# Two attention layers on one core: sums over partitions and the turn of the maxima on VectorE instead of TensorE

## The chip, the cores and the metric

The kernel runs on one core of one Trainium2 chip, as one program. The metric is the device time of one execution in microseconds (us), lower is better. A core has five engines that work beside each other, each through its own instructions in order: TensorE (PE, matrix products, with the weight loads shown as PEld), VectorE (DVE), ScalarE (ACT), GpSimd (POOL) and SyncE (SP), which here issues DMAs. Data lies in SBUF, 128 partitions of a row each; TensorE writes to PSUM, and the other engines read both.

## The reference

Two transformer layers over 1024 latent tokens with 256 context tokens, width 1024. Each normalizes and modulates its input, projects it, runs attention of 16 heads, multiplies by a gate and projects back. Layer 0 has grouped queries (4 key heads), layer 1 latent attention: its queries are expanded from 384 columns, normalized per head (96 columns) and rotated in 32 of them. Cut to what the change touches:

```python
def gqa_attend(q, k, v):
    s = jnp.einsum('bqhgd,bkhd->bhgqk', q, k).astype(jnp.float32) * (GQA_HEAD_DIM ** -0.5)
    p = jax.nn.softmax(s, axis=-1).astype(v.dtype)
    return jnp.einsum('bhgqk,bkhd->bqhgd', p, v)
...
    def q_heads(q_a, n):
        q = (rms_norm(q_a, p["q_a_norm"]) @ p["w_q_b"]).reshape(B, n, MLA_HEADS, MLA_NOPE + MLA_ROPE)
        q = rms_norm(q, p["q_norm"])
        return jnp.split(q, [MLA_NOPE], axis=-1)
```

The softmax needs, for each query, the maximum of its scores and the sum of their exponentials over all keys. Latent queries read 1280 keys, context queries 256.

## The kernel before

`Attention` (L312) runs a layer's units one after another; `run` (L694) is the loop. A unit is one pair of heads' share: 1024 query columns (two halves of 512) against the keys, in tiles `kt` of 128 keys, ten for a latent unit and two for a context unit. Layer 0 (`WIDE`) has 16 latent and 4 context units, the latter fifth, tenth and last two; layer 1 has 16 latent units. Keys lie on the partitions and queries in the columns, so that the exponentials `p` can go straight into the second product.

One unit, step by step:

- For each `kt`, `scores_by_halves` (L560) makes the scores `st` in PSUM in several products, of which the last one adds a shift: minus the query's maximum, taken from a row. ACT takes the exponential, `p` (L567).
- Beside each `kt`, TensorE makes scores of a later unit with the queries on the partitions, `mx` (L436 and L441 in layer 0, one tile of 1024 columns per `kt`; L402 and L412 in layer 1, two tiles of 512). DVE reduces them to a maximum per query (L445, L447; L404, L415), and L465 joins these to `m`, 128 x 8. Layer 0 has two PSUM buffers for `mx`, layer 1 three of half the size.
- `turn` (in `do_shift`, L469 to L481) brings `m` into a row: TensorE transposes it into a buffer of `mx` (L474), DVE copies it to `crow` in SBUF (L476), and two DMAs on SP put it in the row of the shift.
- POOL adds up the tiles `p` over `kt` in `acp` (L601), 128 x 1024; for the last four `kt` of a latent unit DVE first adds pairs (`acd`, L587), and POOL adds those.
- `do_av` (L617) multiplies `p` with the values, 20 products of 2 x 512 columns a latent unit, into `avt` or `av`.
- `total` (in `finish`, L655 to L669) sums `acp` over the partitions: four pairs of products with the constant `twos` (L662) on TensorE, into a buffer of `mx` or `av`; DVE transposes the result (L666) and takes reciprocals (L667), 128 x 8; a DMA writes them to `rrow` in memory, from where `spread` fetches them over the partitions, and POOL multiplies the output with them and with the gate (L681, L682).

A unit's total comes in the following unit: in layer 0 after the first `kt` of that unit's AV (`postponed`, `second`), in layer 1 before its AV. Totals of units that end while context units run are kept until the next latent unit, so two can come at once.

In `run`, a manual schedule keeps PE, DVE and ACT in the order of the code; the framework places POOL's and SP's instructions. Elsewhere the framework orders all engines.

The query stage of layer 1 comes between the two attentions: two `staged` loops (L1833, L1836) of eight steps, one per 128 tokens, with `q_expand` (L1772) in each. For each of two halves of 384 columns it makes the projection `mm`, a sum of squares `qss`, a reciprocal root `q_rs` (L118 on DVE, then POOL), two multiplications from PSUM into `t` (L1788) and `qt` (L1793), an addition on POOL, and the multiplication `t` by `q_rs` (L1796). `q_store` transposes the result on TensorE (`tp`, L1806) and splits it (`tl`, L88) for storing.

Of the kernel before, what the change touches and what calls it, by code (L numbers as in the profile page):

```python
# [10 lines left out]
F32 = mybir.dt.float32  # L11
# [26 lines left out]
def hybrid_kernel(ctx: ExitStack, tc: tile.TileContext, ins: dict, out: bass.AP):  # L38
# [12 lines left out]
    def pad(pool, size):  # L51

        pool.tile([P, size // 4], F32, name="pad", tag="pad", bufs=1)

    pad(sm_pool, 352)

    ident = const.tile([P, P], F32, name="ident")
    make_identity(nc, ident)
# [1 line left out]
    pool.memset(mhalf, -0.5)  # L60
    twos = const.tile([P, 32], F32, name="twos")
    pool.memset(twos, 2.0)


    x1d = dram.tile([NT, D], F32, name="x1d")
# [16 lines left out]
    def in_order(engine):  # L82

        return tc.manual_schedule(engines={engine})

    def split(hi, lo, src):
        act.copy(hi, src)
# [224 lines left out]
    class Attention:  # L312
        def __init__(self, l, units, ops):
            self.l, self.units, self.ops = l, units, ops
            self.state = {}
            self.vcache = {}
            self.kcache = {}
            self.sm = sm_pool
            self.step = 0
            self.deferred = []  # L320
            self.totals = []
            self.turns = []
            self.started = 0
            self.done = 0
            self.todo = []
            self.last_lat = [u for u in units if u["kind"] == "lat"][-1]
# [133 lines left out]
        def do_shift(self, u):  # L460

            s = self.state[id(u)]
            if u["kind"] == "lat":
                m = self.sm.tile([P, 8], F32, name="m1", tag="m1")
                dve.reduce_max(m, s["m"], axis=AX.X)  # L465
            else:
                m = s["m"][:, :, 0]

            def turn():  # L469
                if not WIDE[self.l]:  # L470
                    t = self.ps_m.tile([P, 512], F32, name="mx", tag="mx")[:8, :P]
                else:
                    t = self.ps_m.tile([P, 1024], F32, name="mx", tag="mx")[:8, :P]
                pe.transpose(t, m, ident)  # L474
                r = self.rows[self.units.index(u) % 2] if WIDE[self.l] else self.sm.tile([8, P], F32R, name="crow", tag="crow", bufs=1)
                dve.tensor_copy(r, t)  # L476
                if HALVES[self.l]:
                    for n in range(2):
                        sp.dma_start(raw(s["crow"][n]), raw(r[4 * n:4 * n + 4, :]))
                else:  # L480
                    sp.dma_start(raw(s["crow"]), raw(r))  # L481

            self.turns.append((self.units.index(u), turn))

# [117 lines left out]
                s["sum"] = t  # L602
            s["total"] = ([s["sum"]] if held else []) + last

        def do_av(self, u, group, ps, second=None):

            s = self.state[id(u)]
            kts = u["kts"]
            if group[0] == kts[0]:
                if not WIDE[self.l]:  # L610
                    s["av"] = self.ps_o.tile([P, 512], F32, name="av", tag="av")
                s["v"] = self.load_v(u)
            for kt, p in zip(group, ps):
                if second and kt == kts[1]:
                    second()
                for n in range(2):
                    pe.matmul(s["av"][64 * n:64 * n + 64, :], lhsT=s["v"][:, kt, u["vc"]:u["vc"] + 64],  # L617
                              rhs=p[:, n * 512:(n + 1) * 512], start=kt == kts[0], stop=kt == kts[-1])
            if group[-1] == kts[-1]:
                self.finish(u)  # L620
# [12 lines left out]
        def finish(self, u):  # L633
            l, op, sm = self.l, self.op, self.sm
            s = self.state.pop(id(u))
            lat = u["kind"] == "lat"
            o = op.tile([P, 512], F32, name="os", tag="os")
            act.copy(o, s["av"])

            def parts(dst):  # L640

                if lat:
                    r = slice(64 * u["par"], 64 * u["par"] + 64)
                    return [(slice(64 * n, 64 * n + 64), dst[u["pair"], r, 512 * n:512 * n + 512], lambda t: t)
                            for n in range(2)]
                g = u["g"]
                return [(slice(0, P), dst[2 * g:2 * g + 2, :, NL:].rearrange("a p n -> p a n"),
                         lambda t: t.rearrange("p (a n) -> p a n", a=2))]

            rrow = self.rd.tile([2, 512], F32, name="rrow", tag="rrow")  # L650

            rb = sg = None
            cr = sm.tile([P, 8], F32, name="cr", tag="cr")

            def total(gap):  # L655
                if WIDE[l]:
                    t = self.ps_m.tile([P, 1024], F32, name="mx", tag="mx")[:, :512]
                else:
                    t = s["av"] if u is not self.units[-1] and not HALVES[l] else self.ps_m.tile([P, 512], F32, name="mx", tag="mx")
                for i, part in enumerate(s["total"]):  # L660
                    for q in range(4):
                        pe.matmul(t[32 * q:32 * q + 32, :256], lhsT=twos, rhs=part[:, q * 256:q * 256 + 256],  # L662
                                  start=i == 0, stop=i == len(s["total"]) - 1)

                tr = t[:, 256:]
                dve.transpose(tr, t[:, :256].rearrange("p (a b) -> p b a", b=8))  # L666
                dve.reciprocal(cr, tr.rearrange("p (b a) -> p b a", a=32)[:, :, 0])  # L667
                sp.dma_start(rrow.rearrange("o (a b) -> (o a) b", b=8), cr)
                self.later(*((d + gap, fn) for d, fn in zip(self.ops["gaps"], (spread, scale, store))))  # L669

            def spread():
                nonlocal rb, sg
                rb = op.tile([P, 512], F32, name="rb", tag="rb", bufs=1)
                sg = op.tile([P, 512], F32, name="sg", tag="sg", bufs=1)
                for rows, src, view in parts(sgd[l]):
                    sp.dma_start(view(sg[rows, :]), src)
                for n in range(2):
                    sp.dma_start(rb[64 * n:64 * n + 64, :], rrow[n:n + 1, :].broadcast_to([64, 512]))

            def scale():  # L680
                pool.tensor_mul(rb, rb, sg)  # L681
# [12 lines left out]
        def run(self, lead, ahead, extra, tail):  # L694
# [3 lines left out]
            with tc.manual_schedule(engines={mybir.EngineType.PE, mybir.EngineType.DVE, mybir.EngineType.Activation}):  # L698
                for t, u in enumerate(self.units):
# [18 lines left out]
                    for group in (kts[:cut], kts[cut:]):  # L718
# [30 lines left out]
                            self.add_up(u, *(([], sums) if cut else (sums, [])))  # L749
                        if final:  # L750
                            self.run_deferred(self.step + 2)
                        def sum_totals():
                            gap = 0
                            while self.totals and (whole or late or final):
                                self.totals.pop(0)(gap)
                                gap += 3

                        postponed = WIDE[self.l] and whole and group[0] == kts[0]
                        if not postponed:
                            sum_totals()  # L760
                        if t % 2 and end:
                            if parts:
                                parts()
                            parts = extra.pop(0)() if extra else None
                        self.do_av(u, group, ps, sum_totals if postponed else None)
                        self.step += (2 + len(group)) // 3
                gap = 0
                while self.totals:
                    self.totals.pop(0)(gap)
                    gap += 3  # L770
            self.run_deferred(self.step)

# [521 lines left out]
    def l0_open(at, st):  # L1294
        pool_ = st.enter_context(tc.tile_pool(name="shift0", bufs=1, **right))
        at.minus = pool_.tile([P, 4, P], F32R, name="minus")
        at.shift = pool_.tile([P, 512], F32R, name="shift")
        at.rows = [pool_.tile([8, P], F32R, name=f"crow{i}") for i in range(2)]
        pool.memset(raw(at.shift), 0.0)
        for i in range(4):  # L1300
            a, b = (ident[:, j:j + 1].broadcast_to([P, P]) for j in (i, 64 + i))
# [421 lines left out]
    with ExitStack() as st:  # L1723
# [47 lines left out]

        def q_expand(tt, c, w, lat):  # L1772
            qah, qal = lat
            held = []
            for q4 in range(2):
                ns = slice(384 * q4, 384 * q4 + 384)
                ps = ps_mm.tile([P, 512], F32, name="mm", tag="mm")
# [14 lines left out]
                for s_ in range(2):  # L1792
                    dve.tensor_tensor(t2[:, :, :, s_, :], p5[:, :, :, 1 - s_, :],  # L1793
                                      sv[:, :, s_, :].unsqueeze(1).broadcast_to([P, 4, 2, 8]), op=ALU.mult)
                pool.tensor_add(t1v[:, :, 64:96], t1v[:, :, 64:96], t2.rearrange("p h a s d -> p h (a s d)"))
                dve.tensor_tensor(t1v, t1v, rs.unsqueeze(2).broadcast_to([P, 4, 96]), op=ALU.mult)  # L1796
                held.append(t1)
            return held

        def q_store(tt, c, held):  # L1800
# [29 lines left out]
            return fn  # L1830

        todo_g = list(slices)
        staged(range(TL), q_compress, q_latent, later, expand(0), gate((0, 0, 0, 0, 0, 1, 1, 1)), later, store(0))  # L1833
        wqb.append(load_weight(ins["l1_w_q_b"], 3, 768, 768))
        wg1 = load_weight(w_in1, KT, 1184, 512)
        staged(range(TL), q_fetch, expand(1), gate((0, 1, 0, 1, 0, 1, 1, 1)), store(1))  # L1836
    stQ.close()
    stT.close()
    at.open_early(stE)
# [86 lines left out]
```

## Time and profile before

| | us |
|---|---|
| median of 3 runs | 1669.49 (1668.81 to 1670.78) |
| the profiled execution | 1668.65 |
| its span in the trace | 1666.9 |
| TensorE matmuls L662, `acp`, 272 of them | 21.3 busy |
| TensorE transpositions L474, 36 of them | 9.7 busy |
| VectorE L666, 36 of them | 16.0 busy |
| VectorE L667, 36 of them | 7.5 busy |
| VectorE L476, 36 of them | 9.8 busy |
| VectorE L1796, 32 of them | 20.0 busy, 24.3 idle before them |

A row of the profile's timeline gives the start in us from the span's start, the duration, the engine, the line, the operation and the tiles it writes and reads. A number in brackets is the time for which the engine had been idle before, with what it waited for. Rows of the same kind are merged (x4), and their durations overlap a little at the edges, since an instruction starts before the one ahead has quite ended; what a piece of work takes of its engine is therefore read from start to start. A busy time in the page sums durations.

### The profile page before, as it was taken

How to read it: one execution, taken by the hardware profiler on the slowest of the kernel's cores; microseconds unless marked ns; L12 is line 12 of the kernel's file. 1: busy time of each engine (PE TensorE's matmuls, PEld its weight loads, DVE VectorE, ACT ScalarE, POOL GpSimd, SP SyncE). 2: the span in 40 equal slices, each digit the busy share in tenths (PEclk: the TensorE clock that was granted, in tenths of full speed). 3: DMA queues.
4: the chain of work that ended last, by engine and by line, in shares of the span. 5: the costliest groups of instructions: out<-in, count | busy, mean ns of one | idle time of the engine just before them, and what ended most of it. 6: DMA issues, size and time to landing. Idle time of an engine off the chain costs nothing.

```text
span 1666.9 us, 27267 instructions
## 1 busy us (share of the span) xinstructions
PE 1636.5 (98%) x10236; PEld 1187.3 (71%) x10236; DVE 1043.3 (63%) x1660; ACT 640.1 (38%) x944; POOL 949.1 (57%) x624
## 2 busy tenths in 40 slices
PE   8999999999999999999999999999999999999998
PEld 5776668885555555558888898887676766767587
DVE  3774553457788777625675667755777777677231
ACT  4642222224455544432234543331443534435310
POOL 2673441118899898842235555450767878778521
PEclk9999999999999999999999999999999999999999
DMA  9547856532252432156424776767456564563451
GB/s 311 181 131 251 254 164 197 155 97 59 77 146 69 120 87 77 51 151 208 133 71 131 231 208 189 226 203 195 113 130 157 117 147 112 130 141 73 128 172 68
DMA packets 221116, 244.21 MB, mean 147 GB/s; under 512 B 23160, under 2 KB 160616, under 8 KB 220984
## 3 DMA queue, kind: packets, MB, share of 16 engines
q1 hardware_dynamic: 220560, 242.36, 52.1%
q8 instruction: 81, 1.33, 0.3%
q14 instruction: 51, 0.42, 0.1%
q10 hardware_dynamic: 424, 0.11, 0.0%
HBM read 168.62 MB, written 73.63 MB: 145 GB/s over the span
## 4 chain that ended last, share of the span: by engine, by line
PE 86%; DVE 6%; POOL 3%; issue 3%; ACT 1%; DMA 1%; ACTq 0%; SPq 0%; DVEq 0%; POOLq 0%
PE st L560 19%; PE avt L617 9%; PE av L617 8%; PE mm L94 8%; PE mm L96 7%; PE mm L95 7%; PE mx L402 4%; PE y L94 4%; PE y L96 4%; PE y L95 4%; PE mx L436 2%; PE pm L201 1%; PE mx L662 1%; DVE wb L137 1%; DVE m L445 1%
## 5 line engine op out<-in xcount | busy, mean ns | idle before, releaser
L567 ACT ACTIVATE p<-st 128x1024 f32<-128x1024 f32 x328 | 335.9, 1027 | 155.8 <-PE st L560 140.4
L601 POOL TENSOR_TENSOR acp<-acp,p 128x1024 f32<-128x1024 f32 x128 | 305.4, 2386 | 8.3 <-ACT p L567 0.4
L404 DVE TENSOR_REDUCE m<-mx 128x1 f32<-128x512 f32 x256 | 175.6, 691 | 95.1 <-PE mx L402 89.4
L445 DVE TENSOR_REDUCE m<-mx 128x1 f32<-128x1024 f32 x128 | 150.4, 1219 | 70.3 <-PE mx L436 69.7
L601 POOL TENSOR_TENSOR acp<-p 128x1024 f32<-128x1024 f32 x34 | 81.5, 2399 | 176.5 <-ACT p L567 176.5
L617 PE MATMUL avt<-p,v 128*64 128x512 f32 x672 | 152.5, 598 | 0.6 <-DVE crow L476 0.3
L601 POOL TENSOR_TENSOR acp<-acp,acd 128x1024 f32<-128x1024 f32 x60 | 141.9, 2365 | 14.7 <-DVE acd L587 11.5
L587 DVE TENSOR_REDUCE acd<-p 128x512 f32<-128x1024 f32 x124 | 144.8, 1221 | 6.9 <-ACT p L567 6.9
L617 PE MATMUL av<-p,v 128*64 128x512 f32 x640 | 141.1, 595 | 0.0
L137 POOL TENSOR_TENSOR wb<-wraw,wa 128x512 fp32r<-128x512 f32 (+3 forms) x65 | 87.7, 1364 | 78.3 <-ACT wa L158 78.3
L94 PE MATMUL mm<-wa,hh 128*128 128x512 f32 (+2 forms) x336 | 126.5, 376 | 2.0 <-ACT hh L974 2.0
L560 PE MATMUL st<-QH,KH 64*128 64x512 f32 x320 | 122.7, 407 | 0.1
L96 PE MATMUL mm<-wa,hl 128*128 128x512 f32 (+2 forms) x336 | 121.0, 360 | 1.4 <-DVE hl L977 1.4
L95 PE MATMUL mm<-wb,hh 128*128 128x512 f32 (+2 forms) x336 | 120.4, 358 | 0.0
L560 PE MATMUL st<-QH,KL 64*128 64x512 f32 x320 | 118.3, 391 | 0.0
L560 PE MATMUL st<-QL,KH 64*128 64x512 f32 x320 | 117.8, 390 | 0.0
L94 PE MATMUL y<-wa,oh 128*128 128x512 f32 (+1 forms) x296 | 114.2, 386 | 0.6 <-ACT oh L813 0.6
L95 PE MATMUL y<-wb,oh 128*128 128x512 f32 (+1 forms) x296 | 113.7, 384 | 0.0
L96 PE MATMUL y<-wa,ol 128*128 128x512 f32 (+1 forms) x296 | 113.6, 384 | 0.0
L617 PEld LDWEIGHTS av<-p,v 128*64 128x64 f32 x640 | 44.5, 137 | 88.3 <-issue 87.6
L617 PEld LDWEIGHTS avt<-p,v 128*64 128x64 f32 x672 | 44.9, 136 | 86.9 <-issue 80.6
L94 PE MATMUL mm<-hh,wa 128*128 128x512 f32 (+1 forms) x264 | 103.2, 391 | 0.2 <-DVE qt L1793 0.2
(247 smaller groups left out, 4015.8 us busy)
## 6 DMA issues: line engine op xcount, KB each, us to landing
mraw<-in_l_w_mod SPq DMA_DIRECT2D x64, 256.0 KB
wraw<-in_l_w_in SPq DMA_DIRECT2D x28, 512.0 KB
KH<-k1h SPq DMA_DIRECT2D x32, 320.0 KB
KL<-k1l SPq DMA_DIRECT2D x32, 320.0 KB
rb<-rrow SPq DMA_DIRECT2D x72, 128.0 KB
mraw<-in_l_w_mod SPq DMA_DIRECT2D x16, 512.0 KB
QA<-q0h SPq DMA_DIRECT2D x32, 256.0 KB
wraw<-in_l_w_out SPq DMA_DIRECT2D x16, 512.0 KB
```

The source lines that it names most:

```text
L94: pe.matmul(ps, lhsT=lh(k), rhs=rh(k), start=first and i == 0, stop=False)
L95: pe.matmul(ps, lhsT=lh(k), rhs=rl(k), start=False, stop=False)
L96: pe.matmul(ps, lhsT=ll(k), rhs=rh(k), start=False, stop=last and i == len(ks) - 1)
L137: eng.tensor_sub(lo, a, b)
L402: pe.matmul(held["m"][:, cs], lhsT=q[:, t * P:(t + 1) * P], rhs=k[:, ks], start=j == 0, stop=j == len(pairs) - 1)
L404: dve.reduce_max(s["m"][:, i, n:n + 1], held["m"], axis=AX.X)
L445: dve.reduce_max(s["m"][:, i, 0:1], m, axis=AX.X)
L560: pe.matmul(ps[:, n * 512:(n + 1) * 512], lhsT=lh, rhs=rh, start=j == 0, stop=j == last)
L567: act.activation(p, ps, AF.Exp, scale=self.ops["scale"])
L587: dve.reduce_sum(t[:, ns], p2.rearrange("p a n -> p n a")[:, ns, :], axis=AX.X)
L601: pool.tensor_add(t, a, b)
L617: pe.matmul(s["av"][64 * n:64 * n + 64, :], lhsT=s["v"][:, kt, u["vc"]:u["vc"] + 64], rhs=p[:, n * 512:(n + 1) * 512], start=kt == kts[0], ...
```

## The change

- Two tiles are new, shared by all: `square`, 128 x 32, and `turned`, 128 x 128. A pad of the pool they lie in shrinks by as much. `turn_squares` transposes the four 32 x 32 blocks of `square` (partitions 0, 32, 64 and 96) into 32 partitions of `turned`, side by side.
- `turn` no longer uses TensorE: DVE copies `m` to the first eight columns of `square`, transposes the squares, and the two DMAs read `turned`.
- `total_by_squares` replaces `total` but for the layer's last units (`late` or `final`): DVE reduces `acp` with `apply_transpose` into `square`, transposes the squares, adds the four, doubles, takes reciprocals of 32 x 32, and the DMA reads these. It holds for 17 totals of layer 0 and 15 of layer 1; three and one remain on TensorE.
- Totals come ahead of AV in layer 0 too; `second` and `postponed` go.
- The query stage runs in written order on DVE, and `q_expand` multiplies by `q_rs` behind both halves.

The diff, cut:

```diff
-    pad(sm_pool, 352)
+    pad(sm_pool, 224)
...
+    square = sm_pool.tile([P, 32], F32R, name="square", tag="square", bufs=1)
+    pool.memset(raw(square), 0.0)
+    turned = sm_pool.tile([P, P], F32, name="turned", tag="turned", bufs=1)
...
+    def turn_squares(dst):
+
+        for g in range(4):
+            dve.transpose(dst[:, 32 * g:32 * g + 32], raw(square[32 * g:32 * g + 32, :]))
...
             def turn():
-                if not WIDE[self.l]:
-                    t = self.ps_m.tile([P, 512], F32, name="mx", tag="mx")[:8, :P]
-                else:
-                    t = self.ps_m.tile([P, 1024], F32, name="mx", tag="mx")[:8, :P]
-                pe.transpose(t, m, ident)
-                r = self.rows[self.units.index(u) % 2] if WIDE[self.l] else self.sm.tile([8, P], F32R, name="crow", tag="crow", bufs=1)
-                dve.tensor_copy(r, t)
...
+                at_ = 32 * (self.units.index(u) % 2)
+                r = turned[at_:at_ + 32, :]
+                dve.tensor_copy(square[:, :8], m)
+                turn_squares(r)
+                for n in range(2):
+                    sp.dma_start(raw(s["crow"][n]), r[4 * n:4 * n + 4, :])
...
+            def total_by_squares(gap):
+                part, = s["total"]
+                dve.tensor_reduce(raw(square), part.rearrange("p (b r) -> p b r", r=32), axis=AX.X, op=ALU.add,
+                                  apply_transpose=True)
+                sums = turned[64:96, :]
+                turn_squares(sums)
+                i = self.sums % 4
+                self.sums += 1
+                c = turned[96:128, 32 * i:32 * i + 32]
+                dve.reduce_sum(c, sums.rearrange("q (g r) -> q r g", r=32), axis=AX.X)
+                dve.tensor_scalar(c, c, 2.0, None, op0=ALU.mult)
+                dve.reciprocal(c, c)
+                sp.dma_start(rrow.rearrange("o (a b) -> (o a) b", b=32), c)
+                then(gap)
...
-                        postponed = WIDE[self.l] and whole and group[0] == kts[0]
-                        if not postponed:
-                            sum_totals()
+                        gap = 0
+                        while self.totals and (whole or late or final):
+                            self.totals.pop(0)(gap, not (late or final))
+                            gap += 3
...
-                        self.do_av(u, group, ps, sum_totals if postponed else None)
+                        self.do_av(u, group, ps)
...
                 pool.tensor_add(t1v[:, :, 64:96], t1v[:, :, 64:96], t2.rearrange("p h a s d -> p h (a s d)"))
+                held.append(t1)
+                todo.append((t1v, rs))
+            for t1v, rs in todo:
                 dve.tensor_tensor(t1v, t1v, rs.unsqueeze(2).broadcast_to([P, 4, 96]), op=ALU.mult)
-                held.append(t1)
...
-        staged(range(TL), q_compress, q_latent, later, expand(0), gate((0, 0, 0, 0, 0, 1, 1, 1)), later, store(0))
+        with in_order(mybir.EngineType.DVE):
+            staged(range(TL), q_compress, q_latent, later, expand(0), gate((0, 0, 0, 0, 0, 1, 1, 1)), later, store(0))
```

How the instructions stand on TensorE in an early latent unit of layer 0, from its last scores to the next unit's first maxima (each row: line, operation, output and inputs, shape, how many in a row), before:

```order
L560 MATMUL st<-QL,KA 128x512 x2
L560 MATMUL st<-shift,minus 128x512 x2
L474 MATMUL mx<-ident,m_3758 8x128
L617 MATMUL avt<-p,v 64x512 x2
L662 MATMUL mx<-acp,twos 32x256 x4
L617 MATMUL avt<-p,v 64x512 x18
L436 MATMUL mx<-KA,QA 128x512 x2
```

and with the change:

```order
L563 MATMUL st<-QA,KB 128x512 x2
L563 MATMUL st<-QL,KA 128x512 x2
L563 MATMUL st<-shift,minus 128x512 x2
L618 MATMUL avt<-p,v 64x512 x20
L445 MATMUL mx<-KA,QA 128x512 x2
```

The turn L474 and the total L662 are gone from between the scores and AV, and AV is one stretch of 20.

The same place on DVE, from the maxima of the unit's last scores to those of the next unit, before:

```order
L445 TENSOR_REDUCE m<-mx 128x1 x4
L476 CAST crow_2949<-mx 8x128
L587 TENSOR_REDUCE acd<-p 128x512 x4
L666 STREAM_TRANSPOSE mx<-mx 128x256
L667 RECIPROCAL cr<-mx 128x8
L445 TENSOR_REDUCE m<-mx 128x1 x4
```

and with the change:

```order
L454 TENSOR_REDUCE m<-mx 128x1 x4
L481 CAST square<-m_3763 128x8
L92 STREAM_TRANSPOSE turned<-square 32x32 x4
L590 TENSOR_REDUCE acd<-p 128x512 x4
L661 TENSOR_REDUCE square<-acp 128x32
L92 STREAM_TRANSPOSE turned<-square 32x32 x4
L668 TENSOR_REDUCE turned<-turned 32x32
L669 TENSOR_SCALAR turned<-turned 32x32
L670 RECIPROCAL turned<-turned 32x32
L454 TENSOR_REDUCE m<-mx 128x1 x4
```

Three instructions beside the reductions L445 and L587 have become thirteen, at the same two places: ahead of `acd` and behind it.

In the query stage, one step of `q_expand` on DVE, before (`qss` sums squares, `t` and `qt` are written from the projection `mm`):

```order
L1783 TENSOR_REDUCE qss<-sq 128x4
L1788 TENSOR_TENSOR t_10386<-mm,cwq 128x384
L118 TENSOR_SCALAR q_ms<-qss 128x4
L1793 TENSOR_TENSOR qt_10388<-mm,swq 128x8x8 x2
L1783 TENSOR_REDUCE qss<-sq 128x4
L1796 TENSOR_TENSOR t_10386<-t_10386,q_rs 128x384
L118 TENSOR_SCALAR q_ms<-qss 128x4
L1788 TENSOR_TENSOR t_10411<-mm,cwq 128x384
L1793 TENSOR_TENSOR qt_10413<-mm,swq 128x8x8 x2
```

and with the change:

```order
L1798 TENSOR_REDUCE qss<-sq 128x4
L126 TENSOR_SCALAR q_ms<-qss 128x4
L1803 TENSOR_TENSOR t_10516<-mm,cwq 128x384
L1808 TENSOR_TENSOR qt_10518<-mm,swq 128x8x8 x2
L1798 TENSOR_REDUCE qss<-sq 128x4
L126 TENSOR_SCALAR q_ms<-qss 128x4
L1803 TENSOR_TENSOR t_10540<-mm,cwq 128x384
L1808 TENSOR_TENSOR qt_10542<-mm,swq 128x8x8 x2
L1814 TENSOR_TENSOR t_10516<-t_10516,q_rs 128x384
L1814 TENSOR_TENSOR t_10540<-t_10540,q_rs 128x384
```

The multiplication of the first half by `q_rs` has moved behind the second half's work.

More of the change, by code (lines that the diff above doesn't have):

```diff
@@ L321, in __init__ @@
             self.totals = []
+            self.sums = 0
             self.turns = []
@@ L469, in turn @@
             def turn():
-                if not WIDE[self.l]:
-                    t = self.ps_m.tile([P, 512], F32, name="mx", tag="mx")[:8, :P]
-                else:
-                    t = self.ps_m.tile([P, 1024], F32, name="mx", tag="mx")[:8, :P]
-                pe.transpose(t, m, ident)
-                r = self.rows[self.units.index(u) % 2] if WIDE[self.l] else self.sm.tile([8, P], F32R, name="crow", tag="crow", bufs=1)
[L476 to L481, printed above, removed]
+                at_ = 32 * (self.units.index(u) % 2)
[4 more added lines that the diff above has]
+                    sp.dma_start(raw(s["crow"][n]), r[4 * n:4 * n + 4, :])
             self.turns.append((self.units.index(u), turn))
@@ L603, in add_up, with do_av @@
             s["total"] = ([s["sum"]] if held else []) + last
-        def do_av(self, u, group, ps, second=None):
+        def do_av(self, u, group, ps):
             s = self.state[id(u)]
@@ L613, in do_av @@
             for kt, p in zip(group, ps):
-                if second and kt == kts[1]:
-                    second()
                 for n in range(2):
@@ L653, in finish, with then, total @@
             cr = sm.tile([P, 8], F32, name="cr", tag="cr")
-            def total(gap):
+            def then(gap):
+                self.later(*((d + gap, fn) for d, fn in zip(self.ops["gaps"], (spread, scale, store))))
+            def total_by_squares(gap):
[12 more added lines that the diff above has]
+                then(gap)
+            def total(gap, squares):
+                if squares:
+                    return total_by_squares(gap)
                 if WIDE[l]:
@@ L668, in total @@
                 sp.dma_start(rrow.rearrange("o (a b) -> (o a) b", b=8), cr)
-                self.later(*((d + gap, fn) for d, fn in zip(self.ops["gaps"], (spread, scale, store))))
+                then(gap)
             def spread():
@@ L751, in run @@
                             self.run_deferred(self.step + 2)
[L752 to L756, printed above, removed]
-                        postponed = WIDE[self.l] and whole and group[0] == kts[0]
-                        if not postponed:
-                            sum_totals()
+                        gap = 0
+                        while self.totals and (whole or late or final):
+                            self.totals.pop(0)(gap, not (late or final))
+                            gap += 3
                         if t % 2 and end:
@@ L768, in run @@
                 while self.totals:
-                    self.totals.pop(0)(gap)
+                    self.totals.pop(0)(gap, False)
                     gap += 3
@@ L1297, in l0_open @@
         at.shift = pool_.tile([P, 512], F32R, name="shift")
-        at.rows = [pool_.tile([8, P], F32R, name=f"crow{i}") for i in range(2)]
         pool.memset(raw(at.shift), 0.0)
@@ L1773, in q_expand @@
             qah, qal = lat
-            held = []
+            held, todo = [], []
             for q4 in range(2):
@@ L1832, in hybrid_kernel @@
         todo_g = list(slices)
-        staged(range(TL), q_compress, q_latent, later, expand(0), gate((0, 0, 0, 0, 0, 1, 1, 1)), later, store(0))
+        with in_order(mybir.EngineType.DVE):
+            staged(range(TL), q_compress, q_latent, later, expand(0), gate((0, 0, 0, 0, 0, 1, 1, 1)), later, store(0))
         wqb.append(load_weight(ins["l1_w_q_b"], 3, 768, 768))
         wg1 = load_weight(w_in1, KT, 1184, 512)
-        staged(range(TL), q_fetch, expand(1), gate((0, 1, 0, 1, 0, 1, 1, 1)), store(1))
+        with in_order(mybir.EngineType.DVE):
+            staged(range(TL), q_fetch, expand(1), gate((0, 1, 0, 1, 0, 1, 1, 1)), store(1))
     stQ.close()
```

## The prediction

> **What bounds the kernel now.** I read the page's first parts, then the busy times of the two attention layers, then the timelines of PE, DVE and POOL in one unit of each.
>
> ```profile
> span 1666.9 us, 27267 instructions
> ...
> PE 1636.5 (98%) x10236; PEld 1187.3 (71%) x10236; DVE 1043.3 (63%) x1660; ACT 640.1 (38%) x944; POOL 949.1 (57%) x624
> ...
> PEclk9999999999999999999999999999999999999999
> ...
> PE 86%; DVE 6%; POOL 3%; issue 3%; ACT 1%; DMA 1%; ACTq 0%; SPq 0%; DVEq 0%; POOLq 0%
> ```
>
> TensorE is the bound: 98% busy at a full granted clock, and 86% of the chain. So a PE instruction that goes is worth its time, provided that the engine which takes the work does not become late itself. By stage (a stretch of layer 0's units, one of layer 1's):
>
> ```profile
> core 0: us, PE busy (x) PEld busy (x) DVE busy (x) ACT busy (x) POOL busy (x), PEclk, DMA share, GB/s
> 377.00:737.00 360.00, 356.09 (x2511) 195.03 (x2511) 267.88 (x287) 179.75 (x189) 310.49 (x149) 1.00 0.33 89
> 1150.00:1537.00 387.00, 387.00 (x2930) 271.98 (x2927) 284.34 (x413) 164.10 (x172) 282.26 (x136) 1.00 0.56 128
> ```
>
> DVE is busy 74% in layer 0 and 73% in layer 1, and POOL 86% and 73%. That is room on average only; it has to be looked at unit by unit.
>
> **What the change removes from TensorE.** One unit of layer 0 without a total, one with (the columns: start, duration, instruction), then one of layer 1:
>
> ```profile
> 720.31 0.39 PE L560 MATMUL st<-shift,minus 64*128 64x512 f32 x2
> 720.63 1.94 PE L617 MATMUL avt<-p,v 128*64 128x512 f32 x8
> ```
> ```profile
> 377.06 8.74 PE avt L617 x40
> ```
> ```profile
> 583.91 0.39 PE L560 MATMUL st<-shift,minus 64*128 64x512 f32 x2
> 584.23 0.27 PE L474 MATMUL mx<-ident,m 128*8 128x128 f32 x1
> 584.43 1.08 PE L617 MATMUL avt<-p,v 128*64 128x512 f32 x4
> 585.44 0.64 PE L662 MATMUL mx<-acp,twos 128*32 128x256 f32 x8
> 586.01 7.95 PE L617 MATMUL avt<-p,v 128*64 128x512 f32 x36
> 593.88 0.50 PE L436 MATMUL mx<-KA,QA 64*128 64x512 f32 x2
> ...
> 1540.60 0.27 PE L474 MATMUL mx<-ident,m 128*8 128x128 f32 x1
> 1540.80 0.64 PE L662 MATMUL mx<-acp,twos 128*32 128x256 f32 x8
> 1541.37 8.80 PE L617 MATMUL av<-p,v 128*64 128x512 f32 x40
> ```
>
> From the last score to the first AV takes 0.32 us without a turn and 0.52 (583.91 to 584.43) with one: a turn costs 0.20. AV with a total in its middle takes 9.45 (584.43 to 593.88), unbroken 8.74: a total costs 0.71. In layer 1 the two cost 0.20 and 0.57 (1540.60, 1540.80, 1541.37). The change moves 20 turns and 17 totals of layer 0, and 16 turns and 15 totals of layer 1: 20 x 0.20 + 17 x 0.71 = 16.1, and 16 x 0.20 + 15 x 0.57 = 11.8. At most **28 us** go from PE.
>
> **What it adds to VectorE.** One unit of layer 0 and one of layer 1:
>
> ```profile
> 601.66 0.17 DVE L465 TENSOR_REDUCE m<-m 128x8 f32<-128x16 f32 x1
> 601.74 4.61 DVE L445 TENSOR_REDUCE m<-mx 128x1 f32<-128x1024 f32 x4
> 606.27 0.27 DVE L476 CAST crow<-mx 8x128 fp32r<-8x128 f32 x1
> 606.47 4.68 DVE L587 TENSOR_REDUCE acd<-p 128x512 f32<-128x1024 f32 x4
> 611.07 0.44 DVE L666 STREAM_TRANSPOSE mx<-mx 128x256 f32<-128x256 f32 x1
> 611.55 0.21 DVE L667 RECIPROCAL cr<-mx 128x8 f32<-128x8 f32 x1
> 616.14 1.23 DVE L445 TENSOR_REDUCE m<-mx 128x1 f32<-128x1024 f32 x1 [4.38 <-PE mx L436]
> ...
> 1264.08 1.41 DVE L404 TENSOR_REDUCE m<-mx 128x1 f32<-128x512 f32 x2 [4.47 <-PE mx L402]
> 1265.72 1.40 DVE L404 TENSOR_REDUCE m<-mx 128x1 f32<-128x512 f32 x2 [0.24 <-PE mx L402]
> ...
> 1280.35 0.28 DVE L476 CAST crow<-mx 8x128 fp32r<-8x128 f32 x1
> ...
> 1290.31 1.40 DVE L404 TENSOR_REDUCE m<-mx 128x1 f32<-128x512 f32 x2 [4.48 <-PE mx L402]
> ```
>
> What goes is the cast (606.27 to 606.47, 0.20) and L666 with L667 (611.07 to 611.76, 0.69): 0.89. What comes, per unit:
>
> - The cast to `square` and the small reduce have their nearest row in L465, which holds the engine for 0.08 to 0.17: 0.10 and 0.17. The tensor_scalar: 0.16 at most. The reciprocal: 0.21, as L667.
> - Eight 32x32 transpositions, in two sets of four. L465 shows that a small instruction lets the next begin after 0.08 to 0.11; a set is then 0.44, which is also what L666 takes for 256 columns at once. If each must end before the next starts, it is a set of four times 0.21, 0.84. I take **0.44**, and keep 0.84.
> - The transposing reduction of 128x1024: L587 reads as many elements in 1.17 (4.68 / 4). No row transposes and sums at once. It cannot well be under L587's; as two passes it would be four of L666's on top, 1.76. I take 1.15.
> - Starts between them: 0.15.
>
> Together 0.10 + 0.88 + 1.15 + 0.17 + 0.16 + 0.21 + 0.15 = 2.82, net **1.93** a unit. To that come waits for POOL. The first of these rows is DVE's, the others POOL's:
>
> ```profile
> 982.72 1.25 DVE L118 TENSOR_SCALAR q_ms<-qss 128x4 f32<-128x4 f32 x1
> ...
> 982.50 1.45 POOL L137 TENSOR_TENSOR wb<-wraw,wa 128x512 fp32r<-128x512 f32 x1 [1.77 <-ACT wa L158]
> ...
> 602.77 9.76 POOL L601 TENSOR_TENSOR acp<-acp,p 128x1024 f32<-128x1024 f32 x4
> ...
> 1275.24 7.35 POOL L601 TENSOR_TENSOR acp<-acp,p 128x1024 f32<-128x1024 f32 x3
> 1283.07 4.81 POOL L601 TENSOR_TENSOR acp<-acp,acd 128x1024 f32<-128x1024 f32 x2 [0.48 <-DVE acd L587]
> ```
>
> A tensor_scalar of 128x4, mostly 0.16 long, took 1.25 and ended with POOL's instruction (983.95 and 983.97): DVE copies and scalar operations from SBUF to SBUF wait for a running POOL add, while L465 and L587, which also read SBUF, run beside the adds (601.66 and 606.47, within the POOL rows). The old cast read PSUM; the new one reads `m` in SBUF. At 606.27 POOL's running add has until 607.65 (602.77 + 2 x 2.44): 1.4 us. At 1280.35 it has until 1282.59: 2.2. The tensor_scalar meets the adds of `acd`: between 0 and 2.4; 1.0 in layer 0, where POOL is fuller, and 0.35 in layer 1, where their second one is nearly through. What is queued behind the held instructions is the rest of DVE's unit, and for its maxima PE waits.
>
> *Layer 0.* DVE has 4.38 idle a unit; PE's unit would be 0.91 shorter, so 3.47 is left. Needed: 1.93 + 1.4 + 1.0 = 4.33, over by 0.9. Nothing wins that back: the reductions come one after another without idle time (601.74, four in 4.61, 1.15 each), at PE's own pace. So a unit saves 0.91 and pays 0.9: **0** for the layer.
>
> *Layer 1.* Idle 4.48, less 0.77, is 3.71. Needed: 1.93 + 2.2 + 0.35 = 4.5, over by 0.8. Here there are three buffers of maxima: the fourth maximum of a unit is the first to need a reduction done, some 0.9 late (a kt of 1.64, less a reduction of 0.7), and every kt has 0.24 idle in which the lag is worked off. So the gain is kept, but with thin cover: I take 2 off for units whose cast falls early in an add. **-9.7**.
>
> *Query stage.*
>
> ```profile
> PE tp L1806 <- DVE tl L88: 4.8, 4, 1.8
> ```
>
> PE waits there 4.8 us in all for DVE. Two multiplications by `q_rs` behind both halves no longer stand for POOL's addition between them; but in written order a transposed tile's `tl` can stand behind a wait too. Between -4.8 and +3; I take **-1.5**. The edit of `do_av` costs nothing: it is PE's order alone. The DMAs stay on SP's queue, two for a turn and one for a total, and what a turn's bring is wanted by the next unit's scores, not before 616.14, ten us behind the cast.
>
> The sum is 1668.65 - 0 - 9.7 - 1.5 = 1657.5 against the profiled execution's own time (its span is 1666.9); the median of the runs is 0.84 above that: **1658 us**.
>
> **The rivals.**
>
> *Everything is hidden* (0.17). The cast is not held, or falls where POOL is idle. Then layer 0 needs 1.93 + 1.0 of 3.47 and layer 1 less: 1669.5 - 28 - 1.5 = 1640. For it: the idle 4.4 us of DVE in each unit. Against: POOL is in an add at both places.
>
> *DVE becomes the bound: the squares run one after another* (0.30, **slower**). Each of the four transpositions of a set reads another 32 partitions. At 0.84 a set, a unit needs 0.80 more. In layer 0 nothing absorbs that: 17 x 0.80 = 13.6. In layer 1 the excess is 0.8 + 0.8, over the 0.9 of the buffers by 0.7: 15 x 0.7 = 10.5. That gives 1658 + 24 = 1682. It is slower than before from about 0.37 more a unit (1669.5 - 1658 = 11.5, over 32 units). Against it: L465 is followed after 0.08. [...]
>
> *About even* (0.10). The cast is held longer in layer 1 (it starts with an add, 2.4) and the lag gets through for half of its gain: 1658 + 6 and more, up to 1672.
>
> *The query stage loses* (0.05). A held instruction in written order stops PE's next `tp` in each of the 16 steps by some 0.5: +8, with layer 0 even: 1668 to 1684. A transposing reduction in two passes (+1.76 a unit, over 1700) is in this rest as well, at a few in 100; the range leaves it out.
>
> **How the numbers follow.** The forecast's own case, 1648 to 1666, has 0.38; hidden 0.17; even 0.10; slower by the squares 0.30 and by the rest 0.05. A measurement of this kernel tells about 0.2%, 3.3 us, from no change. Faster: 0.38 + 0.17 = 0.55; same 0.10; slower 0.35. The range, 1643 to 1684, takes in the serial squares, and leaves out most of the hidden case and the two-pass reduction. As both signs hold much, the likeliest case's own range is 1648 to 1666.
>
> **What would show it.** In the changed kernel's profile: the gap from the last score to AV at 0.3, and AV unbroken at 8.7 (the 28 us). The cast to `square` at over 1 us in most units, ending with a POOL add: the waits; at 0.2, the hidden case. A set of squares as a group of four lasting 0.44 or 0.84. The reduction with `apply_transpose` at 1.15. DVE's idle time before a unit's first maximum near nothing in layer 0, with PE waiting for `m` there; some idle left in layer 1. Wrong would be: PE waits in layer 1, or a time within 3 us of before.

## The result, and the profile after

The changed kernel takes 1696.6 us (median of three runs, 1694.8 to 1700.6) against 1670.1 for the kernel before, measured beside it: a ratio of 1.0162, interval 1.0136 to 1.0188. A fourth run took 2284 us at a granted clock of 0.655 and is left out as disturbed. The changed kernel is **slower by 27 us**; the forecast was 12 faster, and the range ended at 1684. The profiled execution took 1696.63.

The page of the changed kernel, its span, busy times and the TensorE clock:

```profile
span 1694.8 us, 26922 instructions
...
PE 1625.4 (96%) x9944; PEld 1188.9 (70%) x9944; DVE 1195.0 (71%) x1996; ACT 640.9 (38%) x944; POOL 952.6 (56%) x625
...
PEclk9999999999999999989999999999999999999999
```

TensorE has 11 us less work, although part of it ran at a lower clock (0.988 on average, 1.000 before), and DVE 152 us more. What TensorE waited for (the view of waits: who for whom, us in all, times, the longest):

```profile
PE mx L445 <- DVE m L454: 28.9, 13, 5.9
PE st L563 <- DMA shift<-turned: 8.7, 1, 8.7
PE mx L683 <- POOL acp L604: 5.0, 1, 5.0
```

None of these three waits was of any size before (L436 for L445: one wait of 1.2). Where they stand is best seen by place. The table gives how much later (+) or earlier (-) than in the profile of before a unit's last AV product ends, worked out from the starts and durations of these products in the traces; the units are counted from one, and the fifth, the tenth and the last two are context units. The AV of unit 18 comes in two parts, 24 products and 16, with scores between them.

| end of | changed kernel |
|---|---|
| layer 0, unit 1 | -1.4 |
| unit 5 | -2.4 |
| unit 6 | +2.3 |
| unit 8 | +12.6 |
| unit 10 | +13.0 |
| unit 12 | +18.4 |
| unit 17 | +22.4 |
| unit 18 (last latent), first part | +21.0 |
| unit 18, second part | +32.3 |
| layer 1, first AV | +31.7 |
| layer 1, last AV | +20.5 |
| span | +27.9 |

So there are three losses and one gain. Layer 0's units lose 24 us, in jumps behind the context units (+15 from unit 5 to 8, +5 from 10 to 12). One wait at the end of layer 0 loses 11. Layer 1 gains 11.2, nearly all of the 11.8 that the prediction took from TensorE there. The end of the program loses 7.

DVE in an ordinary unit of layer 0, with the additions of `acd` in the middle:

```profile
603.75 0.32 DVE L481 CAST square<-m 128x8 fp32r<-128x8 f32 x1
604.11 0.84 DVE L92 STREAM_TRANSPOSE turned<-square 32x32 f32<-32x32 f32 x4
604.99 4.69 DVE L590 TENSOR_REDUCE acd<-p 128x512 f32<-128x1024 f32 x4
609.60 1.23 DVE L661 TRANSPOSE_TENSOR_REDUCE square<-acp 128x32 f32<-128x1024 f32 x1
610.87 0.85 DVE L92 STREAM_TRANSPOSE turned<-square 32x32 f32<-32x32 f32 x4
611.75 0.37 DVE L668 TENSOR_REDUCE turned<-turned 32x32 f32<-32x128 f32 x1
612.16 1.62 DVE L669 TENSOR_SCALAR turned<-turned 32x32 f32<-32x32 f32 x1
613.81 0.35 DVE L670 RECIPROCAL turned<-turned 32x32 f32<-32x32 f32 x1
614.19 4.62 DVE L454 TENSOR_REDUCE m<-mx 128x1 f32<-128x1024 f32 x4
```

The idle time ahead of a unit's first maximum, 4.38 before, is nil: L454 starts at 614.19 right behind the reciprocal. The turn takes 1.24 (603.75 to 604.99) and the total 4.59 (609.60 to 614.19), 5.8 where 0.9 stood. The longest of the new instructions here, the tensor_scalar, ends with the first of two additions on POOL:

```profile
611.35 4.85 POOL L604 TENSOR_TENSOR acp<-acp,acd 128x1024 f32<-128x1024 f32 x2
```

Half of 4.85 behind 611.35 is 613.78, and 612.16 + 1.62 is 613.78 too. So it is over the whole trace: 31 of the 32 tensor_scalars end 0.04 to 0.05 us behind the end of an instruction of POOL, and the one that met none took 0.18. Of the 36 casts L481 28 end 0.03 to 0.04 us behind an instruction of POOL, and the other eight took 0.16 to 0.17.

In the unit behind a context unit two totals come at once, and the first maximum waits for both:

```profile
581.14 1.23 DVE L661 TRANSPOSE_TENSOR_REDUCE square<-acp 128x32 f32<-128x1024 f32 x1
...
583.70 1.73 DVE L669 TENSOR_SCALAR turned<-turned 32x32 f32<-32x32 f32 x1
...
585.84 1.25 DVE L661 TRANSPOSE_TENSOR_REDUCE square<-acp 128x32 f32<-128x1024 f32 x1
...
588.41 1.87 DVE L669 TENSOR_SCALAR turned<-turned 32x32 f32<-32x32 f32 x1
590.32 0.35 DVE L670 RECIPROCAL turned<-turned 32x32 f32<-32x32 f32 x1
```

That is 9.5 us (581.14 to 590.67) in one stretch. The second loss, in the rows of TensorE and of SP's queue:

```profile
737.76 0.40 PE L563 MATMUL st<-QL,KA 64*128 64x512 f32 x2
746.84 0.94 PE L563 MATMUL st<-shift,minus 64*128 64x512 f32 x2 [8.68 <-DMA shift<-turned]
747.40 0.80 PE L563 MATMUL st<-QA,KA 64*128 64x512 f32 x2
...
736.37 0.31 SPq L671 DMA_DIRECT2D rrow<-turned  x1
736.78 0.45 SPq L697 DMA_DIRECT2D sg<-sgd  x1
737.27 1.23 SPq L707 DMA_DIRECT2D od<-os  x2
738.54 0.60 SPq L697 DMA_DIRECT2D sg<-sgd  x1
739.25 1.17 SPq L699 DMA_DIRECT2D rb<-rrow  x2
740.52 1.14 SPq L798 DMA_DIRECT2D oraw<-od  x2
741.76 2.57 SPq L484 DMA_DIRECT2D shift<-turned  x4
```

The turned maxima of the last two context units were ready at 732.2 (DVE's last square), and the product that adds the shift could have run at 738.2, but their four DMAs stand behind those of the next total, whose reciprocal came at 736.3. In the kernel before, the framework had put them ahead. Behind the gap TensorE runs at half its pace (0.80 for a pair that takes 0.40). The windows, with the granted clock as the third figure from the end:

```profile
738.00:747.00 9.00, 0.32 (x3) 0.19 (x2) 0.00 (x0) 0.00 (x0) 8.69 (x6) 0.77 0.71 190
747.00:753.00 6.00, 6.00 (x28) 5.05 (x30) 2.40 (x2) 3.14 (x4) 3.42 (x2) 0.50 0.34 87
```

The third loss, at the end of layer 1 (POOL, then TensorE):

```profile
1581.69 2.36 POOL L604 TENSOR_TENSOR acp<-acp,p 128x1024 f32<-128x1024 f32 x1
1586.58 1.29 POOL L702 TENSOR_TENSOR rb<-rb,sg 128x512 f32<-128x512 f32 x1 [2.54 <-DMA rb<-rrow]
1587.95 1.29 POOL L703 TENSOR_TENSOR os<-os,rb 128x512 f32<-128x512 f32 x1
1589.19 8.69 POOL L604 TENSOR_TENSOR acp<-acp,p 128x1024 f32<-128x1024 f32 x3
...
1597.93 1.08 PE L683 MATMUL mx<-acp,twos 128*32 128x256 f32 x8 [4.95 <-POOL acp L604]
```

In POOL's order, which the framework makes, the scaling of the last but one unit (which waits for a DMA) now stands in the middle of the last unit's additions, and the last total waits for these.

### The profile page after: what moved, and what is told of

Its sections match the earlier page's. It is cut to its first block, busy times and chain, and to the rows that moved or that the text cites. A ratio compares the mean times of both kernels' runs of the same rounds, so it can differ in the third digit from the quotient of the medians.

```text
span 1694.8 us, 26922 instructions
## 1 busy us (share of the span) xinstructions
PE 1625.4 (96%) x9944; PEld 1188.9 (70%) x9944; DVE 1195.0 (71%) x1996; ACT 640.9 (38%) x944; POOL 952.6 (56%) x625
## 5 line engine op out<-in xcount | busy, mean ns | idle before, releaser
L454 DVE TENSOR_REDUCE m<-mx 128x1 f32<-128x1024 f32 x128 | 149.0, 1217 | 17.8 <-PE mx L445 17.5
L590 DVE TENSOR_REDUCE acd<-p 128x512 f32<-128x1024 f32 x124 | 145.3, 1234 | 16.2 <-ACT p L570 15.3
L604 POOL TENSOR_TENSOR acp<-acp,acd 128x1024 f32<-128x1024 f32 x60 | 142.5, 2375 | 21.6 <-DVE acd L590 18.4
L702 POOL TENSOR_TENSOR rb<-rb,sg 128x512 f32<-128x512 f32 x36 | 46.5, 1291 | 105.2 <-DMA rb<-rrow 75.9
```

Source lines behind the costliest of these rows:

```text
L454: dve.reduce_max(s["m"][:, i, 0:1], m, axis=AX.X)
L590: dve.reduce_sum(t[:, ns], p2.rearrange("p a n -> p n a")[:, ns, :], axis=AX.X)
L604: pool.tensor_add(t, a, b)
```

## The experiments

**The query stage alone.** The kernel before with the last two parts of the diff (`in_order` around both loops, `q_rs` behind both halves).

> The kernel before with the edit of the query stage alone. By the changed kernel's trace, the stretch from layer 0's last AV to layer 1's first one is 0.6 us shorter than before, so: 1669 us, within 0.2% of before. A rival that blames the written order for part of the loss expects 1672 or more.

Measured: 1665.7 us, ratio 0.9989 (0.9979 to 0.9999). The written order costs nothing and gains perhaps 2 us; it is no part of the loss.

**Turns by squares alone, totals by squares alone.** Each is the changed kernel without the other part and without the query stage's edit.

```diff
-                            self.totals.pop(0)(gap, not (late or final))
+                                self.totals.pop(0)(gap, False)
```
```diff
-                dve.tensor_copy(square[:, :8], m)
-                turn_squares(r)
+                    t = self.ps_m.tile([P, 1024 if WIDE[self.l] else 512], F32, name="mx", tag="mx")[:8, :P]
+                    pe.transpose(t, m, ident)
+                    dve.tensor_copy(r, t)
```

> The kernel before with the turns by squares alone, totals on TensorE. Theory 'VectorE has room, and what decides is the length of all that is added to a unit': a unit gets 0.85 for the squares and up to 2 for a held cast, less 0.2, and has 4.2 idle, so all is hidden; 36 turns of 0.20 go from TensorE: 1662 us. Theory 'held casts cost by themselves': each unit gets about 1 us longer, 1690. The DMAs of the last two context units' turns should be ahead of the reciprocals' on SP, with no gap of 8.7 us.

> The kernel before with the totals by squares alone, turns on TensorE (VectorE copies the row to another tile than before). Room theory: a total adds 1.27 + 0.88 + 0.41 + 0.2 to 1.9 + 0.38 - 0.69 = 2.4 to 4.2 where 3.7 is idle, so single totals are hidden or nearly, double ones lose about 4 each: layer 0 about -5, layer 1 -8.5, the late additions on POOL at the end up to +5: 1657 to 1669. If instead the totals alone are what makes VectorE late in every unit of layer 0, as in the changed kernel: 1680 and more.

Measured: turns 1663.2 (0.9973, interval 0.9962 to 0.9984), totals 1669.7 (1.0008, 0.9997 to 1.0019). Neither is slower, and in the changed kernel both together cost 27. In the turns' run DVE still has idle time behind the turn, although the cast is held for 1.17:

```profile
602.69 1.17 DVE L481 CAST square<-m 128x8 fp32r<-128x8 f32 x1
603.90 0.85 DVE L92 STREAM_TRANSPOSE turned<-square 32x32 f32<-32x32 f32 x4
...
612.44 4.79 DVE L454 TENSOR_REDUCE m<-mx 128x1 f32<-128x1024 f32 x4 [2.36 <-PE mx L445]
```

So a held copy cost nothing here, where 2.36 us of room are left behind it. Of the two predicted amounts, 1662 and 1657 to 1669, the first was met within 1.2, and the second missed by 0.7. By place, the totals' run loses 5.0 from unit 5 to 8 and gains 3.1 from unit 12 to 17: there single totals pay, and the first pair does not.

**Layer 1 alone.** Turns and totals by squares where `not WIDE[self.l]`, with the query stage's edit.

> The change in layer 1 and the query stage alone; layer 0 as before. By place: layer 1's units -11.3, query stage -0.6, the wait of the last total for POOL at the end +7: 1664.5 us. If that wait at the end is an effect of layer 0 or of SP's order there: 1657. If layer 1's gain depends on layer 0's lag: 1669 or more.

Measured: 1659.0, ratio 0.9951 (0.9936 to 0.9966), between the two sums. Layer 1's units gain 10.1 by place (-2.3 at its first AV, -12.4 at its last), and the wait for POOL at the end is there, but with 2.7 us instead of 5.0, so less was lost than was put down for it. Layer 1's gain needs nothing of layer 0.

**Without the scalar operation.** The same result, with each sum read twice:

```diff
-                dve.reduce_sum(c, sums.rearrange("q (g r) -> q r g", r=32), axis=AX.X)
-                dve.tensor_scalar(c, c, 2.0, None, op0=ALU.mult)
+                dve.tensor_reduce(c, sums.rearrange("q (g r) -> q r g", r=32).unsqueeze(3).broadcast_to([32, 32, 4, 2]), axis=AX.XY, op=ALU.add)
```

> The changed kernel, with the doubling done by the small reduction (it reads each sum twice) instead of a tensor_scalar; the result is the same. Theory 'the held tensor_scalar decides in layer 0': it takes 1.7 us there, the longer reduction gives back 0.3, and TensorE's waits of 29 us for the maxima fall to below 8: 1676 us. [...]

Measured: 1665.8, ratio 0.9979 (0.9965 to 0.9993): one instruction of 32 x 32, 32 times, was worth 31 us. The groups of the changed kernel, and behind the dots of this one (line, operation, count, busy us, mean ns):

```profile
L669 DVE TENSOR_SCALAR turned<-turned 32x32 f32<-32x32 f32 x32 | 32.0, 1000 | 1.1
L668 DVE TENSOR_REDUCE turned<-turned 32x32 f32<-32x128 f32 x32 | 12.0, 375 | 1.1
...
L668 DVE TENSOR_REDUCE turned<-turned 32x32 f32<-32x256 f32 x32 | 13.2, 412 | 1.1
L669 DVE RECIPROCAL turned<-turned 32x32 f32<-32x32 f32 x32 | 11.2, 349 | 1.1
```

Reading twice as much costs 0.04 us; the hold does not pass to the reciprocal, which stays at 349 ns. The gain is larger than expected, since layer 0's units lose 3.6 instead of 24 (+1.9 at unit 1, +5.5 at unit 17), and the other two losses shrink as well: the late row costs about 9 instead of 11.3, and the end 0.3 instead of 7.4, although POOL's order there is that of the changed kernel.

**The late DMAs, two attempts.** First the DMAs of the last two context units' turns on ScalarE, then SP in written order through layer 0's attention.

```diff
-                    sp.dma_start(raw(s["crow"][n]), r[4 * n:4 * n + 4, :])
+                    (act if WIDE[self.l] and self.units.index(u) > 17 else sp).dma_start(raw(s["crow"][n]), r[4 * n:4 * n + 4, :])
```
```diff
-            with tc.manual_schedule(engines={mybir.EngineType.PE, mybir.EngineType.DVE, mybir.EngineType.Activation}):
+            with tc.manual_schedule(engines={mybir.EngineType.PE, mybir.EngineType.DVE, mybir.EngineType.Activation} | ({mybir.EngineType.SP} if WIDE[self.l] else set())):
```

> The changed kernel, with the DMAs of the turns of layer 0's last two units issued by ScalarE instead of SyncE. Theory 'they stand behind the reciprocals' DMA on SP': the gap of 8.7 us goes, and with it the 2.5 us in which TensorE ran at half its pace behind it: 1687 us. If the row itself is late (VectorE): 1697.

> The changed kernel, with SyncE's DMAs of layer 0's attention in written order, which puts the turns of the last two context units ahead of the reciprocals' DMA; nothing else. Moving these DMAs to ScalarE had left the gap, since they still came behind other DMAs there. Theory 'the order on SP makes the row late': the gap of 8.7 us goes and the half pace behind it: 1687 us. Rival 'the row is late by itself, because VectorE is': the squares of both turns end 5 us ahead of the scores that want them, so at most 1 us of wait may remain by it; if more remains, this theory falls.

Measured: 1702.7 (1.0203, 1.0174 to 1.0233) and 1698.8 (1.0175, 1.0152 to 1.0198). The first missed altogether: the DMAs were issued from 741.8 on, no earlier than on SP, behind a wait of ScalarE for something that this run does not name, and the gap was 8.8. In the second the local expectation held: between the two parts of unit 18's AV nothing is lost (+35.4 and +35.5), where the changed kernel lost 11.3. The total did not follow, since in written order other loads come late:

```profile
PE mx L445 <- DVE m L454: 25.9, 9, 7.9
PE mx L445 <- DMA QA<-q0h: 6.9, 4, 4.1
```

So the late row was a matter of order among the DMAs, and a fixed order for all of SP is no remedy. Order is not all of it: in runs in which VectorE has less to do, TensorE waited less there, 6.5 us without the scalar operation and, further below, 5.3 without holds and 2.5 in the best version.

**The last but one total of layer 1 on TensorE.**

```diff
-                            self.totals.pop(0)(gap, not (late or final))
+                            self.totals.pop(0)(gap, not (late or final or (u is self.last_lat and not WIDE[self.l])))
```

> The changed kernel, with the total of layer 1's last but one unit on TensorE again; POOL's additions for the last unit then stand ahead of the scaling that waits for this total. Theory 'POOL's order at the end costs 5 us, and the slow stretch behind it 2': 1691 us. Rival 'POOL is late there by itself': 1697.

Measured: 1697.0, ratio 1.0177 (1.0133 to 1.0221), by its median no different from the changed kernel (1696.6). By place it does what was expected: the delay is +23.8 at layer 1's last AV and +23.8 at the end, without the 7.4 between them, and POOL's last four additions are together again:

```profile
1583.60 9.72 POOL L604 TENSOR_TENSOR acp<-acp,p 128x1024 f32<-128x1024 f32 x4
1595.54 1.36 POOL L702 TENSOR_TENSOR rb<-rb,sg 128x512 f32<-128x512 f32 x1 [2.22 <-DMA rb<-rrow]
```

Layer 0 happened to lose 3 more in this execution (+25.7 at unit 17). The runs of kernels in which DVE is late there spread by 6 us and more, so the end's 7 us are shown by the trace, not by the times. And the order costs this only where the last totals come late: the run without the scalar operation kept it and lost 0.3.

**What a set of squares takes.** Layer 1's change alone, with a second set behind each turn's, into a part of `turned` that nothing reads then:

```diff
                     turn_squares(r)
+                    for g in range(4):
+                        dve.transpose(turned[64:96, 32 * g:32 * g + 32], raw(square[:32, :]))
```

> Layer 1's change alone, with a second set of four transpositions behind each turn's, which all read partitions 0 to 31 and write a scratch area that nothing reads. If a transposition waits for the one ahead because it reads other partitions, this set takes 0.45 where the turn's own takes 0.85. If each of them takes 0.21 whatever it reads, it takes 0.85 too. The time as in the layer 1 run, within 3 us.

One run: 1660.1 us. The two sets in DVE's timeline:

```profile
1197.71 0.84 DVE L92 STREAM_TRANSPOSE turned<-square 32x32 f32<-32x32 f32 x4
1198.59 0.48 DVE L485 STREAM_TRANSPOSE turned<-square 32x32 f32<-32x32 f32 x4
```

0.48 where all four read partitions 0 to 31, 0.84 where each reads others. The change gets about the upper of the two values that the prediction had kept: its 68 sets of four took 0.84 to 0.86 each.

**Without holds.** The run without the scalar operation, and the reduction that joins the maxima writes `square` itself:

```diff
-                dve.tensor_copy(square[:, :8], m)
+                dve.reduce_max(square[:, :8], m, axis=AX.X)
```

> The changed kernel without a tensor_scalar and without a cast: the reduction that joins the maxima writes the square itself, and the small sum reads each value twice; the result is the same. [...] Rival 'a reduction that writes SBUF waits as well': 1666 or more.

Measured: 1660.5, ratio 0.9959 (0.9944 to 0.9974). In place of a cast of 727 ns on average stands

```profile
L480 DVE TENSOR_REDUCE square<-m 128x8 fp32r<-128x16 f32 (+2 forms) x36 | 6.1, 170 | 0.9
```

and layer 0's units gain 8.0 (+1.5 to -6.5), pairs of totals and serial squares and all.

**Pairs of totals on TensorE**, in the changed kernel:

```diff
-                            self.totals.pop(0)(gap, not (late or final))
+                            self.totals.pop(0)(gap, one and not (late or final))
```

with `one = len(self.totals) < 2` ahead of the loop.

> The changed kernel, with the totals that come two at once (two times in layer 0, four totals) on TensorE again; everything else as in the changed kernel, so also the tensor_scalar and the late DMAs. Theory 'the two pairs of totals make most of layer 0's loss': the stretches around them, from the fifth to the eighth and from the tenth to the twelfth AV, lost 20 us in the changed kernel and lose at most 4 here; the other units keep losing 1 us each: 1681 us. Rival 'each unit of layer 0 loses alike': 1696.

Measured: 1677.9, ratio 1.0061 (1.0042 to 1.0081). The two stretches lose 5.5 (unit 5 to 8) and nothing (10 to 12), instead of 15 and 5.4. All of layer 0's units lose 12.1 (-0.85 at unit 1, +11.25 at unit 17) instead of 23.8: four totals of 17 made half of its loss. What is left of the first stretch is the step from unit 5 to 6 (5.7 here, 4.7 in the changed kernel). It comes ahead of the pair: DVE has two turns and a single total there without a break, and TensorE waits 3.2 us.

**The best of it.** Without holds, pairs on TensorE, and also the total that comes in a layer's last latent unit.

```diff
+                            self.totals.pop(0)(gap, one and not (late or final or u is self.last_lat))
```

> As the run without holds; and two totals that come at once, and the totals that come in a layer's last latent unit, stay on TensorE. Layer 0: turns -4, single totals 13 x 0.71 = -9; layer 1: -11.3 + 0.6; query stage -2; the order on SP and POOL at the ends as before: 1642 us. If VectorE's room in layer 0 is too small for turn and total even without holds (3.0 added to 3.5 idle): 1652.

Measured: **1653.9 us, ratio 0.9918 (0.9903 to 0.9933)**, faster than both kernels. It is 12 short of the 1642. Layer 0 gives 12.5 from unit 1 to the first part of unit 18, nearly the 13 summed; layer 1 gives 10.5. The query stage gave 0.2 of the 2 put down. The rest was lost where nothing had been put down: unit 1 ended 3.9 later than in the profile of before (why is not known), and the last context units' row still came 2.5 us late, where 3.9 were lost (-8.6 to -4.7). That the time lies near the 1652 of the other theory is chance, since layer 0 had the room. DVE is 93% busy in layer 0 and TensorE waits for it 0.9 us:

```profile
380.00:702.00 322.00, 319.99 (x2224) 181.29 (x2220) 301.00 (x397) 168.64 (x177) 293.30 (x141) 1.00 0.33 88
```

## Why the prediction was wrong

- **What goes from TensorE** was right: 0.77 a unit in layer 1 came out as 11.2 over the layer, and in the best version layer 0 gives 12.5.
- **The step that failed first: "So a unit saves 0.91 and pays 0.9: 0 for the layer."** Layer 0's units lost 23.8 us in place of 0. The prediction priced one ordinary unit and took it for all 17. Four of the totals come in pairs, and there DVE gets 9.5 us in one stretch. With the pairs on TensorE the loss fell to 12.1. The trace of before had shown the pairs; the prediction did not look at these units apart. The other half lies in the units with two turns and a total at one place, and in the ordinary ones.
- **The ordinary unit was sized too low.** Added were 5.8, not 2.82 and 2.4 of waits: a set of squares 0.85 instead of 0.44, the reciprocal 0.35 instead of 0.21, the small reduction 0.37 instead of 0.17, the tensor_scalar 1.62 to 1.72 instead of 1.16 with its wait; the cast's wait of 1.4 was too high (the whole cast took 0.32 to 1.18 from unit 12 to 17). The sum exceeds the room by 5.8 - 0.9 - 3.5 = 1.4, not 0.9, with the shortest of these casts, and by 2.3 with the longest; less the 0.9 saved on TensorE, a unit should lose 0.5 to 1.4. The last five ordinary units lost 0.8 each net (18.4 to 22.4).
- **The held instructions were there.** That copies and scalar operations from SBUF to SBUF wait for POOL was concluded from one row of 1.25 us, and the changed kernel bears it out for the two forms that it adds: 31 of 32 tensor_scalars of 32 x 32 and 28 of 36 casts of 128 x 8 end with an instruction of POOL (within 0.05 us behind it). It does not hold for every form: a tensor_scalar of 128 x 1 took 0.14 in the middle of one of POOL's subtractions (968.80 in the profile of before, the subtraction from 968.03 to 970.61). Why some forms wait is shown by no run. The tensor_scalar turned out as the dearest of the added small instructions, and a way to write the same sum without it was there. The prediction took the wait as given instead of asking which of the added operations are held.
- **The rival with serial squares** had its price from the upper value, four times 0.21; that the four would run one after another was the author's estimate, which no row of before showed. The changed kernel measured 0.84 to 0.86 a set, and the extra set 0.48 where all four read partitions 0 to 31. So the value was right, but the squares alone do not make the kernel slower: the run without holds has the same squares (272 transpositions of 202 ns on average, as in the changed kernel) and is faster than before (ratio 0.9959). What they cost in time was not tried: no run has the change with quicker squares.
- **Layer 1** kept its gain, with 1.5 more than the 9.7 put down.
- **"The DMAs stay on SP's queue"** was wrong in the end: that what a turn brings is wanted ten us later holds for ordinary units, but the last two context units are short, their row is wanted 6 us after it is ready (732.2 and 738.2), and the framework had put four DMAs behind one that waits. That cost 11.3 us, for which the sum had nothing.
- **The end** was not in the sum either: POOL's changed order costs 7.4 in the changed kernel, and 0.3 where the totals come earlier.
- Both of these waits are dearer than their length. A gap of 8.7 us on TensorE was followed by a granted clock of 0.50 for 6 us (747 to 753), and behind the one of 5.0 it was 0.58 over 6 us (1598 to 1604). In layer 0 it fell at shorter waits too: the clock was 0.50 from 456.15 to 462.98, at a wait of 3.2 us, and from 514.18 to 517.59, at one of 2.45.
- **The query stage** was right within a few us: the run with it alone gains 2.6 between layer 0's last AV and layer 1's first, where 1.5 was put down, the changed kernel 0.6.

The causes do not add up one by one: the scalar operation alone was worth 31 us and the pairs 19, of 27 lost, since with a DVE that is less late all three losses shrink together. How much of that is the clock, which was at 0.50 to 0.58 at the waits named, was not separated. Open is why the framework orders SP and POOL otherwise at the two ends, and what ScalarE waited for with the DMAs.

## What to carry to other kernels

Moving work to an engine with idle time pays as long as it fits into the idle time of each single period: price the worst period (here two totals at once) and not the mean, and add what the instructions wait for, not only what they take. Among operations with the same result choose one that does not wait for another engine's running instruction: here a reduction of 0.17 us instead of a cast of 0.73, and one of 0.41 instead of a sum of 0.375 and a scalar operation of 1.0. When a change alters what the planner schedules, read the order of the queues that it sets at the ends of stages, where the slack of a steady loop is missing.

## What the runs showed of the hardware

- A tensor_scalar of 32 x 32 in SBUF took 1.0 us on average beside POOL's additions (0.18 without one running, 0.20 to 0.23 where one was just ending), a cast of 128 x 8 0.73 (0.16 to 0.17 in the eight that did not end with POOL). Reductions from SBUF to SBUF in their place took 0.17 on average (mostly 128 x 16 to 128 x 8, the run without holds) and 0.41 (32 x 256 to 32 x 32, the run without the scalar operation). In the changed kernel the sum of 32 x 128 took 0.38 inside an addition of POOL (426.69, POOL from 426.37 to 428.77), and the reciprocal of 32 x 32 took 0.35 beside the next (428.84, POOL from 428.85 to 431.20).
- Summing 128 x 1024 with a transposition took 1.23 us, little more than the 1.17 that a sum alone took per 1024 columns (L590, 4.69 for four).
- A reduction over a value read twice (32 x 256 instead of 32 x 128) took 0.41 instead of 0.375.
